# Loading the relative-position buckets of a decoder trunk: six wide transfers between weight units in place of twenty-four narrow ones

## The chip, the cores and the metric

The kernel runs on one core of a Trainium2 chip. A core has five engines with queues of their own: TensorE (PE in the profile; PEld is its weight load), VectorE (DVE), ScalarE (ACT), GpSimd (POOL) and SyncE (SP), which here only issues transfers. Transfers run on 16 DMA engines. The metric is the device time of one execution in microseconds; lower is better.

## The reference, cut to what matters

Two decoder layers run over 256 positions of width 1024, in float32. Layer 0 has differential attention with a relative-position bias, layer 1 latent attention; each is followed by a gated feed-forward part with a short convolution and by a gated embedding. The change touches the bias of layer 0 and two blocks of constants:

```python
bucket = t5_bucket(p_blk[:, :, None] - pos[:, None, :])      # 32 buckets
bias = jnp.take(rel_table, bucket, axis=0).astype(f32)       # table 32 x 8 heads
sc = jnp.where(causal_mask(i, s), sc + bias, NEG_INF)
```

For every pair of a query and a key a bucket number from 0 to 31 picks a row of a table with one value per head.

## The kernel before, in words

All weights lie in one array of units of 128 partitions x 1024 float32 (512 KB), in the order of use. `fetch` (L218) issues the next unit on SP's queue into a ring of five tiles (`st`, BUF_ST = 5). `split_unit` (L232) makes of each unit a high part (`wh`, ScalarE, L240) and the rest (`wl`, VectorE or GpSimd in turn, L241); four such pairs are held (BUF_W = 4). Every product is then three TensorE passes, hi*hi, hi*lo and lo*hi (`mm3`, L195 to L199). Counted from 0, units 0 and 1 are fetched in halves at the start; units 0 to 11 serve `proj_a(0)` and `proj_a(1)`, two units for each of q, k and v of a pair of heads; units 12 to 17 serve `proj_a(2)`, 18 to 23 `proj_a(3)`. The two tiles of `first_stats` (L656, from `in_xn`) take two places in the same ring, behind unit 3.

The bias: `bias_prep` (L377) computes the bucket numbers, 128 queries x 256 keys and 128 x 128, as bfloat16 and stores them in two arrays in DRAM, `s0` and `s1` (L421, L422). `bias_loads` (L435) reads them back as six pieces `oh` of 128 partitions x 2048 bfloat16 (512 KB): partition group j, 32 partitions, holds 4 KB of bucket numbers of query group j, the same in each of the 32 partitions. That is four transfers a piece, 24 in all (L445), each from one 4 KB row to 32 partitions. `bias_mm` (L448) compares each piece with the partition's own number (VectorE, L453), so that each partition marks its bucket, and multiplies with the table: 3 x 96 small products on TensorE (L460), copied to `bias` by ScalarE (L466). `attn_a` reads `bias` from its first head on.

Order: the program is traced in one order, in which `weave` mixes bias and attention with the projections by estimated TensorE time, and `later` runs a step once such an estimate has passed. A planner then orders each engine's queue: of what its own timeline holds ready it takes what was traced first. An engine takes its queue in that order and waits at the head of it. The constants of the convolutions (`cst[:, C_CONV[0]:]`, L668, 176 KB) and `grow` (L816, 384 KB) have no producer on the chip, so the planner put both on SP's queue early. The first are used in the feed-forward part of layer 0 (from L733 on), the second in layer 1.

Of the kernel before, what the change touches and what calls it, by code (L numbers as in the profile page):

```python
# [11 lines left out]
BF16 = mybir.dt.bfloat16  # L12
# [7 lines left out]
P = 128  # L20
# [26 lines left out]
C_CONV = (514, 690)  # L47
# [9 lines left out]
LAG = 6.0  # L57
# [38 lines left out]
def trunk(ctx, tc, xT, xN, pT, pos, consts, grow, wall, out):  # L96
    nc = tc.nc
# [4 lines left out]
    act = ctx.enter_context(tc.tile_pool(name="act", bufs=1))  # L102
# [50 lines left out]
    def later(lag, fn):  # L153
        late.append((clk[0] + lag, fn))
# [56 lines left out]
    cst = cp.tile([P, NCONST], F32, name="cst")  # L211
# [4 lines left out]
    turn = [0.0]  # L216
    share = [SH_A]

    def fetch(pieces=1):
        st = ring.tile([P, UNIT], F32, tag="st", name="st", bufs=BUF_ST)  # L220
        u, n = unit_no[0], UNIT // pieces
        unit_no[0] += 1
        for j in range(pieces):
            nc.sync.dma_start(st[:, j * n:(j + 1) * n], wall[u, :, j * n:(j + 1) * n])
            if pieces > 1:
                yield st
        if pieces == 1:
            yield st
# [19 lines left out]
    for i in range(2):  # L248
        pieces = fetch(2)
        for k in (4 * i, 4 * i + 2):  # L250
            nc.sync.dma_start(hT[:, k:k + 2], xT[:, k:k + 2])
            st = next(pieces)
# [131 lines left out]
    bst = {}  # L384

    def bias_prep():
        tb = []
        rest = col(C_REL, 32)
        for i in range(3):
            bt = ap_.tile([P, 32], BF16, name=f"tb{i}")  # L390
            V.tensor_copy(bt, rest)
            tb.append(bt)
            if i < 2:
                nr = ap_.tile([P, 32], F32, name=f"tr{i}")
                V.tensor_sub(nr, rest, bt)
                rest = nr
        bi = ap_.tile([P, 1], F32, name="bi")
        bidx = ap_.tile([P, 1], I32, name="bidx")
        G.iota(bidx, pattern=[[0, 1]], base=0, channel_multiplier=1)
        V.tensor_scalar(bidx, bidx, 31, None, ALU.bitwise_and)  # L400
        V.tensor_copy(bi, bidx)
        V.tensor_copy(posf, posi)

        identb = ap_.tile([P, P], BF16, name="identb")
        V.tensor_copy(identb, ident)
        dist = ap_.tile([P, 384], BF16, name="dist")
        V.tensor_scalar(dist[:, :S], posf[:, :S], posf[:, S:S + 1], 128.0, ALU.subtract, ALU.min)
        V.tensor_scalar(dist[:, S:], posf[:, P:S], posf[:, S + 1:S + 2], 128.0, ALU.subtract, ALU.min)
        pb = bankB()
        for j in range(len(THRESH) + 1):  # L410
            ge = ap_.tile([P, 384], BF16, tag="ge", name="ge", bufs=4)
            if j == 0:
                V.tensor_scalar(ge, dist, 0.0, 16.0, ALU.max, ALU.min)
            else:
                V.tensor_scalar(ge, dist, float(THRESH[j - 1]), None, ALU.is_ge)
            T.matmul(pb[:, :384], lhsT=identb, rhs=ge, start=j == 0, stop=j == len(THRESH))
        bkb = ap_.tile([P, 384], BF16, name="bkb")
        A.copy(bkb, pb[:, :384])
        s0 = dp.tile([P, S], BF16, name="s0")
        s1 = dp.tile([P, P], BF16, name="s1")  # L420
        nc.sync.dma_start(s0, bkb[:, :S])  # L421
        nc.sync.dma_start(s1, bkb[:, S:])  # L422
        bst["pcs"] = []
        later(LAG, lambda: bias_loads(s0, s1))
        bst["tb"], bst["bi"] = tb, bi
        ld = small(2)
        lscr = a_tile()
        for j in range(2):
            V.tensor_tensor_reduce(lscr[:, j * 64:(j + 1) * 64], col(C_LAM + 128 * j, 64),
                                   col(C_LAM + 128 * j + 64, 64), 1.0, 0.0, ALU.mult, ALU.add, ld[:, j:j + 1])  # L430
        le = small(2)
        A.activation(le, ld, AF.Exp)
        V.scalar_tensor_tensor(neglam, le[:, 1:2], -LAM_INIT, le[:, 0:1], ALU.add, ALU.subtract)

    def bias_loads(s0, s1):  # L435
        for kt, half in ((0, 0), (0, 1), (1, 0)):
            nq = 256 if kt == 0 else 128
            src = s0 if kt == 0 else s1
            ipp = 2048 // nq
            for pc in range(2):  # L440
                oh = act.tile([P, ipp, nq], BF16, tag="og", name="oh", bufs=8)
                i0 = half * 16 + pc * ipp
                row = src.rearrange("(j i) q -> j i q", i=32)[:, i0:i0 + ipp]
                for j in range(4):
                    nc.sync.dma_start(oh[j * 32:(j + 1) * 32], row[j:j + 1].broadcast_to([32, ipp, nq]))  # L445
                bst["pcs"].append(oh)

    def bias_mm():  # L448
        tb, bi = bst["tb"], bst["bi"]
        for n, (kt, half) in enumerate(((0, 0), (0, 1), (1, 0))):  # L450
            pcs = bst["pcs"][2 * n:2 * n + 2]
            for oh in pcs:
                V.tensor_scalar(oh, oh, bi, None, ALU.is_equal)  # L453
            yield 0.0
            for g in range(2):
                ps = bankB()
                for i in range(16):
                    lh = pcs[i // 8][:, i % 8, g * P:(g + 1) * P] if kt == 0 else pcs[g][:, i, :]
                    for z in range(3):
                        T.matmul(ps[:, i * 32:(i + 1) * 32], lhsT=lh, rhs=tb[z], start=z == 0, stop=z == 2)  # L460
                qt = g if kt == 0 else 1
                k0 = half * 16 if kt == 0 else g * 16
                off = 0 if qt == 0 else P + kt * P
                for j in range(4):
                    dst = bias[:, :, off + j * 32 + k0:off + j * 32 + k0 + 16]
                    A.activation(dst, ps.rearrange("p (i j h) -> p j h i", i=16, j=4)[:, j], AF.Copy, scale=-1.0)  # L466
                yield 1.2
        for off in (0, 2 * P):
            v = bias[:, :, off:off + P]
            G.affine_select(out=v, in_=v, pattern=[[0, HA], [-1, P]], compare_op=ALU.is_ge, fill=BIG, base=0,  # L470
                            channel_multiplier=1)
# [193 lines left out]

    run(proj_a(0))
    run(proj_a(1))
    nc.sync.dma_start(cst[:, C_CONV[0]:], consts[:, C_CONV[0]:])  # L668

    def ple_p(l):  # L670
        pst = d_tile()
# [136 lines left out]
    tabs = {}  # L808

    def layer_b_tables():  # L810
        bp = bctx.enter_context(tc.tile_pool(name="bpool", bufs=1))
        tabs["bp"] = bp
        bigm = bp.tile([P, 384], F32, name="bigm")
        tabs["bigm"] = bigm
        tabs["grow"] = bp.tile([P, 768], F32, name="grow")
        nc.sync.dma_start(tabs["grow"], grow)  # L816
        G.memset(bigm, 0.0)
        for off in (0, 2 * P):
            v = bigm[:, off:off + P]
            G.affine_select(out=v, in_=v, pattern=[[-1, P]], compare_op=ALU.is_ge, fill=BIG, base=0,  # L820
                            channel_multiplier=1)
        gqpe = bp.tile([P, 64], F32, name="gqpe")
        V.tensor_scalar(gqpe, col(C_QPE, 64), -SCALE_B, None, ALU.mult)
        ang = d_tile(64)
        for t in range(NT):
            V.tensor_scalar(ang[:, t * 32:(t + 1) * 32], col(C_FREQ, 32), posf[:, S + t:S + t + 1], None, ALU.mult)
        kk = d_tile(64)
        magic = 12582912.0
        V.tensor_scalar(kk, ang, 1.0 / (2.0 * math.pi), magic, ALU.mult, ALU.add)
        V.tensor_scalar(kk, kk, magic, None, ALU.subtract)  # L830
        c1 = 6.28125
        c2 = 0.00193500518798828125
        c3 = 2.0 * math.pi - c1 - c2
        for c in (c1, c2, c3):
            V.scalar_tensor_tensor(ang, kk, -c, ang, ALU.mult, ALU.add)
        V.tensor_scalar(ang, ang, math.pi, -math.pi, ALU.min, ALU.max)
        sn = d_tile(64)
        cs = d_tile(64)
        A.activation(sn, ang, AF.Sin)
        A.activation(cs, ang, AF.Sin, scale=0.5)  # L840
        V.tensor_mul(cs, cs, cs)
        V.tensor_scalar(cs, cs, -2.0, 1.0, ALU.mult, ALU.add)
        for nm, g in (("k", col(C_KPE, 64)), ("q", gqpe)):
            a = bp.tile([P, NT, 64], F32, name=f"ra{nm}")
            b = bp.tile([P, NT, 64], F32, name=f"rb{nm}")
            for t in range(NT):
                c_, s_ = cs[:, t * 32:(t + 1) * 32], sn[:, t * 32:(t + 1) * 32]
                V.tensor_mul(a[:, t, :32], g[:, :32], c_)
                V.tensor_mul(a[:, t, 32:], g[:, 32:], c_)
                V.scalar_tensor_tensor(b[:, t, :32], g[:, 32:], -1.0, s_, ALU.mult, ALU.mult)  # L850
                V.tensor_mul(b[:, t, 32:], g[:, :32], s_)
            tabs[nm] = (a, b)
# [13 lines left out]
    st = {}  # L866
# [417 lines left out]
```

## Time and profile before

| | us |
|---|---|
| median of 3 runs | 787.5 (785.61 to 788.36) |
| the profiled execution, its whole time | 789.36 |
| its span, first to last instruction | 787.6 |
| TensorE busy | 761.2 |
| VectorE busy | 561.2 |
| ScalarE busy | 483.8 |
| GpSimd busy | 296.0 |

The whole time of the profiled execution is 1.76 us more than its span and 1.86 us more than the median of the three runs. TensorE is the engine with the least idle time; the mean granted share of its clock over the span is 0.983. An instruction's row gives its start and its length in us, and in brackets how long its engine stood idle before it and which instruction or transfer ended that wait.

### The profile page before, as it was taken

Reading aid. Unit: us, or ns where it says so; the run is one execution under the profiler, and the core shown is the slowest. Engines: PE = TensorE matmul, PEld = TensorE weight load, DVE = VectorE, ACT = ScalarE, POOL = GpSimd, SP = SyncE. Lnnn points to the kernel's source line nnn. Section 1 sums busy time; section 2 is a strip of 40 time slices with the busy share of each in tenths; the row PEclk is TensorE's granted clock in tenths of the full one; section 3 lists DMA queues with packets and bytes.
Section 4 is the critical chain, followed back from the end, with each engine's and each line's share of the span. In section 5 each row is a group of like instructions: output and inputs, shape, how many; then the busy total and the mean of one; then the engine's idle time right before and its main releaser. Section 6 shows DMA issues by size and latency. Waiting matters only on the chain.

```text
span 787.6 us, 16504 instructions
## 1 busy us (share of the span) xinstructions
PE 761.2 (97%) x6396; PEld 748.7 (95%) x6396; DVE 561.2 (71%) x1142; ACT 483.8 (61%) x1040; POOL 296.0 (38%) x200
## 2 busy tenths in 40 slices
PE   8979999999999999998999899999899999999997
PEld 7979999999999999997989899999899999999997
DVE  6574888659978795538588987975558778775535
ACT  6535887666866665447766777564656666655443
POOL 2653355352332501145835646322523332301151
PEclk9989999999999999998999999999899999999999
DMA  8993345255656675554444323343455566565641
GB/s 310 256 273 100 108 148 162 81 187 161 191 185 191 191 240 197 180 169 134 153 143 135 107 81 108 108 133 108 146 156 188 182 187 184 171 202 176 184 130 55
DMA packets 37519, 127.97 MB, mean 162 GB/s; under 512 B 4672, under 2 KB 6208, under 8 KB 37440
## 3 DMA queue, kind: packets, MB, share of 16 engines
q1 hardware_dynamic: 36720, 126.38, 51.7%
q8 instruction: 50, 0.82, 0.4%
q10 hardware_dynamic: 720, 0.53, 0.2%
q14 instruction: 29, 0.24, 0.1%
HBM read 125.75 MB, written 1.15 MB: 161 GB/s over the span
## 4 chain that ended last, share of the span: by engine, by line
PE 83%; DVE 6%; DMA 4%; ACT 3%; POOL 2%; issue 2%; SPq 0%; POOLq 0%; ACTq 0%; DVEq 0%
PE pa L197 17%; PE pa L198 17%; PE pa L199 17%; PE pc L198 8%; PE pc L199 8%; PE pc L197 8%; DMA oh<-s 2%; DMA st<-in_wall 1%; POOL wl L241 1%; PE pb L198 1%; DVE wl L241 1%; PE pb L197 1%; PE pc L193 1%; PE pb L199 1%; PE pb L525 1%
## 5 line engine op out<-in xcount | busy, mean ns | idle before, releaser
L240 ACT CAST wh<-st 128x1024 fp32r<-128x1024 f32 x221 | 231.0, 1049 | 189.7 <-issue 68.0
L241 POOL TENSOR_TENSOR wl<-st,wh 128x1024 fp32r<-128x1024 f32 x74 | 180.4, 2438 | 245.8 <-ACT wh L240 226.3
L241 DVE TENSOR_TENSOR wl<-st,wh 128x1024 fp32r<-128x1024 f32 x147 | 189.8, 1291 | 87.2 <-ACT wh L240 86.9
L197 PE MATMUL pa<-hgH,wh 128*128 128x256 f32 x504 | 144.2, 286 | 2.2 <-ACT hgH L206 2.2
L198 PE MATMUL pa<-hgL,wh 128*128 128x256 f32 x504 | 144.2, 286 | 0.5 <-DVE hgL L207 0.3
L199 PE MATMUL pa<-hgH,wl 128*128 128x256 f32 x504 | 143.8, 285 | 0.0
L197 PE MATMUL pa<-wh,hgH 128*128 128x256 f32 x328 | 95.4, 296 | 7.4 <-DVE d L348 5.6
L197 PEld LDWEIGHTS pa<-hgH,wh 128*128 128x128 f32 x504 | 97.9, 194 | 2.6 <-ACT hgH L206 2.6
L198 PEld LDWEIGHTS pa<-hgL,wh 128*128 128x128 f32 x504 | 97.9, 194 | 1.1 <-DVE hgL L207 1.1
L199 PEld LDWEIGHTS pa<-hgH,wl 128*128 128x128 f32 x504 | 97.9, 194 | 0.0
L198 PE MATMUL pa<-wl,hgH 128*128 128x256 f32 x328 | 95.2, 291 | 1.2 <-DVE wl L241 0.6
L197 PE MATMUL pa<-og,wh 128*128 128x256 f32 x336 | 95.3, 287 | 0.0
L199 PE MATMUL pa<-wh,hgL 128*128 128x256 f32 x328 | 94.6, 290 | 0.5 <-DVE hgL L204 0.5
L198 PE MATMUL pa<-og,wh 128*128 128x256 f32 x336 | 95.1, 284 | 0.0
L199 PE MATMUL pa<-og,wl 128*128 128x256 f32 x336 | 94.9, 283 | 0.0
L198 PE MATMUL pc<-hgL,wh 128*128 128x256 f32 x328 | 93.8, 286 | 0.6 <-DVE hgL L207 0.5
L197 PE MATMUL pc<-hgH,wh 128*128 128x256 f32 x328 | 94.0, 287 | 0.1
L199 PE MATMUL pc<-hgH,wl 128*128 128x256 f32 x328 | 93.4, 285 | 0.0
L296 POOL TENSOR_TENSOR ssq<-ssq,d 128x256 f32<-128x256 f32 x35 | 33.6, 961 | 132.2 <-ACT d L295 131.7
L197 PEld LDWEIGHTS pa<-wh,hgH 128*128 128x128 f32 x328 | 63.9, 198 | 8.9 <-ACT bias L466 5.7
L198 PEld LDWEIGHTS pa<-wl,hgH 128*128 128x128 f32 x328 | 64.7, 197 | 2.1 <-DVE wl L241 1.0
L199 PEld LDWEIGHTS pa<-wh,hgL 128*128 128x128 f32 x328 | 64.6, 197 | 0.8 <-DVE hgL L204 0.7
(301 smaller groups left out, 1932.7 us busy)
## 6 DMA issues: line engine op xcount, KB each, us to landing
st<-in_wall SPq DMA_DIRECT2D x225, 512.0 KB, 3.6
oh<-s SPq DMA_DIRECT2D x24, 128.0 KB, 5.0
hT<-in_x SPq DMA_DIRECT2D x4, 256.0 KB, 4.8
st<-in_wall SPq DMA_DIRECT2D x4, 256.0 KB, 4.9
st<-in_xn SPq DMA_DIRECT2D x2, 512.0 KB, 6.9
d<-in_p SPq DMA_DIRECT2D x2, 256.0 KB, 4.0
out_h<-hT SPq DMA_DIRECT2D x4, 128.0 KB, 2.0
out_h<-hT ACTq DMA_DIRECT2D x4, 128.0 KB, 2.0
```

The source lines that it names most:

```text
L193: T.transpose(o, i, ident)
L197: T.matmul(ps, lhsT=aH, rhs=bH, start=start, stop=False)
L198: T.matmul(ps, lhsT=aH, rhs=bL, start=False, stop=False)
L199: T.matmul(ps, lhsT=aL, rhs=bH, start=False, stop=stop)
L240: A.copy(hi, st)
L241: eng.tensor_sub(lo, st, f(hi))
L296: G.tensor_add(sq, sq, t)
L525: T.matmul(pss[e][:, a:b], lhsT=x[rows, j, t * P:(t + 1) * P], rhs=y[rows, j, :b - a], start=start, stop=stop)
```

## The change

Each of the six pieces is loaded by one transfer instead of four: 128 partitions as destination, and as source four rows of 4 KB, each repeated 32 times. The pieces are no longer loaded by an estimated time: the fetches of units 12, 13 and 14 each call for two pieces, and `tc.issue_after` puts these on SP's queue behind that unit's transfer. `bias_mm` gives way in the trace until its pieces have been called for, so the first projection of `proj_a(2)` now stands ahead of it. The two blocks of constants are bound behind a unit's transfer in the same way: the convolutions' behind unit 18 (the 19th), `grow` behind the unit that was fetched last when `layer_b_tables` is traced, in the feed-forward part of layer 0.

```diff
     def fetch(pieces=1):
...
         for j in range(pieces):
-            nc.sync.dma_start(st[:, j * n:(j + 1) * n], wall[u, :, j * n:(j + 1) * n])
+            lastfetch[0] = nc.sync.dma_start(st[:, j * n:(j + 1) * n], wall[u, :, j * n:(j + 1) * n]).ins
+            if u in hooks:
+                hooks.pop(u)()
...
-        later(LAG, lambda: bias_loads(s0, s1))
+        for n, (kt, half) in enumerate(((0, 0), (0, 1), (1, 0))):
+            hooks[12 + n] = lambda src=(s0, s1)[kt], kt=kt, half=half: bias_loads(src, kt, half)
...
+    def bias_loads(src, kt, half):
+
+        nq = 256 if kt == 0 else 128
+        ipp = 2048 // nq
+        for pc in range(2):
+            oh = act.tile([P, ipp, nq], BF16, tag="og", name="oh", bufs=8)
+            i0 = half * 16 + pc * ipp
+            row = src.rearrange("(j i) q -> j i q", i=32)[:, i0:i0 + ipp]
+            with tc.issue_after(lastfetch[0]):
+                nc.sync.dma_start(oh.rearrange("p i q -> p (i q)"),
+                                  row.rearrange("j i q -> j (i q)").unsqueeze(1).broadcast_to([4, 32, 2048]))
+            bst["pcs"].append(oh)
+
+    def late_loads(dst, src):
+        with tc.issue_after(lastfetch[0]):
+            nc.sync.dma_start(dst, src)
...
         for n, (kt, half) in enumerate(((0, 0), (0, 1), (1, 0))):
+            while len(bst["pcs"]) < 2 * n + 2:
+                yield None
...
-    nc.sync.dma_start(cst[:, C_CONV[0]:], consts[:, C_CONV[0]:])
+    hooks[18] = lambda: late_loads(cst[:, C_CONV[0]:], consts[:, C_CONV[0]:])
...
-        nc.sync.dma_start(tabs["grow"], grow)
+        late_loads(tabs["grow"], grow)
```

## Rows read from the trace of the kernel before

**Rows 1.** The page: busy time of the engines, and packets of the transfers.
```profile
PE 761.2 (97%) x6396; PEld 748.7 (95%) x6396; DVE 561.2 (71%) x1142; ACT 483.8 (61%) x1040; POOL 296.0 (38%) x200
DMA packets 37519, 127.97 MB, mean 162 GB/s; under 512 B 4672, under 2 KB 6208, under 8 KB 37440
```

**Rows 2.** Stretches: length, PE, PEld, DVE, ACT, POOL busy, granted clock, DMA share, GB/s.
```profile
10.00:15.00 5.00, 4.54 (x37) 3.98 (x35) 4.16 (x20) 2.34 (x7) 0.00 (x0) 1.00 1.02 404
15.00:20.00 5.00, 3.50 (x22) 2.38 (x22) 3.72 (x13) 3.99 (x7) 3.56 (x1) 1.00 0.89 322
...
35.00:40.00 5.00, 5.00 (x45) 5.00 (x43) 1.23 (x2) 3.17 (x4) 1.59 (x2) 1.00 0.88 230
...
55.00:60.00 5.00, 2.55 (x12) 2.58 (x13) 3.84 (x5) 2.40 (x11) 3.93 (x2) 0.50 0.68 215
```

**Rows 3.** The chain of waits, 5 to 75 us: start, us, what.
```profile
29.27 6.13 DMA oh<-s
...
44.84 7.41 DMA st<-in_wall
...
53.40 3.31 DVE wl L241
56.70 0.61 DVE d L348
...
58.01 0.21 PE pa L198
...
61.17 0.12 PE pa L198
...
69.02 0.88 PE pb L525 x6
```

**Rows 4.** Instructions in order of time, 40 to 75 us.
```profile
47.76 1.05 ACT L240 CAST wh<-st 128x1024 fp32r<-128x1024 f32 x1 [8.40 <-DMA st<-in_wall]
...
48.85 1.23 DVE L241 TENSOR_TENSOR wl<-st,wh 128x1024 fp32r<-128x1024 f32 x1 [0.36 <-ACT wh L240]
...
49.31 2.55 PE L460 MATMUL pb<-tb,oh 128*128 128x32 bf16 x96
...
50.05 0.75 DVE L453 TENSOR_SCALAR oh<-oh,bi 128x2048 bf16<-128x2048 bf16 x1
...
57.45 0.55 PE L197 MATMUL pa<-wh,hgH 128*128 128x256 f32 x1 [5.58 <-DVE d L348]
```

**Rows 5.** SP's queue in order of time, 0 to 75 us.
```profile
26.95 1.79 SPq L224 DMA_DIRECT2D st<-in_wall  x2
28.80 12.75 SPq L445 DMA_DIRECT2D oh<-s  x20
41.70 0.35 SPq L224 DMA_DIRECT2D st<-in_wall  x1
...
44.30 27.88 SPq L224 DMA_DIRECT2D st<-in_wall  x9
```

**Rows 6.** GpSimd in order of time, 25 to 40 us.
```profile
28.70 2.40 POOL L241 TENSOR_TENSOR wl<-st,wh 128x1024 fp32r<-128x1024 f32 x1
33.03 2.41 POOL L241 TENSOR_TENSOR wl<-st,wh 128x1024 fp32r<-128x1024 f32 x1 [1.93 <-ACT wh L240]
```

**Rows 7.** VectorE in order of time, 25 to 40 us.
```profile
31.17 1.22 DVE L241 TENSOR_TENSOR wl<-st,wh 128x1024 fp32r<-128x1024 f32 x1 [1.71 <-ACT wh L240]
```

**Rows 8.** Transfers by line: count, KB each, median us from issue to landing.
```profile
st<-in_wall SPq DMA_DIRECT2D x225, 512.0 KB, 3.6
oh<-s SPq DMA_DIRECT2D x24, 128.0 KB, 5.0
```

**Rows 9.** The pieces' own instructions: ns min/median/max, first and last start.
```profile
L453 DVE TENSOR_SCALAR oh<-oh,bi x6: 737/752/2283, 36.6 to 50.0; 128x2048 bf16<-128x2048 bf16 x6
```

**Rows 10.** TensorE in order of time, 14 to 21 us: its waits.
```profile
15.32 0.39 PE L197 MATMUL pa<-wh,hgH 128*128 128x256 f32 x1 [0.78 <-ACT wh L240]
...
19.91 0.39 PE L198 MATMUL pa<-wl,hgH 128*128 128x256 f32 x1 [0.55 <-POOL wl L241]
```

More of the change, by code (lines that the diff above doesn't have):

```diff
@@ L217, in trunk @@
     share = [SH_A]
+    hooks, lastfetch = {}, [None]
     def fetch(pieces=1):
@@ L433, in bias_prep @@
         V.scalar_tensor_tensor(neglam, le[:, 1:2], -LAM_INIT, le[:, 0:1], ALU.add, ALU.subtract)
[L435 to L446, printed above, removed]
+    def bias_loads(src, kt, half):
[12 more added lines that the diff above has]
+            nc.sync.dma_start(dst, src)
     def bias_mm():
```

## The prediction

> **What bounds the kernel now.** I read the page first: TensorE is busy 761.2 us of a span of 787.6 [rows 1], so a change off TensorE gains only where TensorE stands idle or runs at a low clock. The TensorE rows in order of time show where that is near this change: the one long wait of the first 75 us is 5.58 us ahead of the products at 57.45 [rows 4]. Next I read the granted clock by stretches: 0.50, the 1.2 GHz level, from 55 to 60 against 1.00 before [rows 2]; it fell in that wait, and the first products behind it take 0.21 us a step, those from 61.17 on 0.12 [rows 3]. Last, the chain of waits says why: the pieces' transfers, then a weight unit that took 7.41 us to land, its subtraction on VectorE (3.31) and behind that an evacuation (0.61) for which TensorE waited [rows 3]. The same delay is seen on ScalarE, which stood 8.40 us for the transfer of unit 12 before its cast at 47.76 [rows 4].
>
> SP's queue gives the reason. It issued units 10 and 11 from 26.95, then twenty of the pieces' transfers from 28.80 to 41.55, and only then unit 12; units from 13 on follow at 44.30 [rows 5]. Unit 12's place in the ring was free long before: it takes that of unit 7, whose subtraction ended at 28.70 + 2.40 = 31.10 [rows 6]. The 24 narrow transfers took 15 us of the queue, and in that stretch the DMA engines were busy 0.88 of the time for 230 GB/s, while weights and inputs ran at 404 GB/s [rows 2].
>
> **The change part by part, against the profiled execution (789.36 us whole, span 787.6; the median of the runs is 1.86 lower, so differences are carried over to 787.5).**
>
> *What goes.* Unit 12 ahead of the pieces takes away the wait of 5.58 and the half clock. From 57.45 eighteen steps ran before full speed; at 0.21 to 0.22 for 0.12 a step, 3.95 us in place of 2.15, that is 1.8. So 7.4 us can go. Also 18 issues go from SP's queue; SP only issues, so this counts only through what lands sooner.
>
> *What is added: the wide transfers' own time.* A packet here is 4 KB (a partition's row of a unit or of a piece). At 404 GB/s and share 1.02, an engine moves 404 / 16.3 = 24.8 GB/s, 165 ns a packet; in the pieces' stretch 230 / 14.1 = 16.3 GB/s, 251 ns [rows 2]. A wide transfer has 128 packets. How they are dealt to engines no row shows. All transfers before were dealt to 16: the profile lists 276, and of the 4672 packets under 512 B [rows 1] 256 are data (128 rows of 44 B, 128 of 256 B), which leaves 4416 = 16 x 276 completion marks. But each of these has 128 or 32 as its outermost count on both sides; the new source has 4, each row repeated 32 times, against 128 partitions. So the bounds are: 16 engines with 8 packets each (1.3 us at 165, 2.0 at 251) and 4 engines with one row's 32 copies each (5.3 us, 8.0). I take 4 engines, since what both sides can be cut into without cutting the source's outer dimension is 4, and 165 ns, since four engines draw only 99 GB/s, below the 230 that the pieces reached. The outer count decides, I think, and there the 24 old transfers are no near row.
>
> A rule of the Trainium skill bears on this (DMA: Bandwidth & Descriptors, section "Why a DMA increments its semaphore by 16 and not by 1"): the number of engines is the largest up to 16 that divides the slowest dimension of both access patterns, and on such queues they are the lowest-numbered ones. By it the new transfer has 4 engines; the trace agrees as far as it goes, with 16 marks for each transfer of 128 or 32 rows, and has no outer count of 4.
>
> *Where that time lies.* With five ring tiles unit 12 issues at 31.1, unit 13 behind unit 8's subtraction (31.17 + 1.22 = 32.4 [rows 7]), unit 14 behind unit 9's (33.03 + 2.41 = 35.4 [rows 6]). The pieces stand between them: two behind each. A unit lands 3.6 us after issue [rows 8], 1.3 of it packets; I put 1.15 of the rest ahead and 1.15 behind. On the four engines, each in order: unit 12 until 33.6; pieces 1 and 2 (2 x 5.3) until 44.2; unit 13 until 45.5, landed 46.7; pieces 3 and 4 until 56.1, landed 57.2; unit 14 landed 58.5; piece 5 landed 63.8, piece 6 69.1; unit 15 landed 70.5. So each unit now waits for pieces on a quarter of the engines.
>
> TensorE is through with units up to 11 at about 49.5 (its first third of the bias products starts at 49.31 [rows 4]). Units 12 and 13: 48 steps of 0.12, until 55.3. First bias products (2.55 [rows 4]): 57.8. Second: compare 0.75 [rows 9] behind 57.2, idle 0.2, until 60.5. Unit 14: cast 1.05 and subtraction 1.23 [rows 4] behind 58.5, idle 0.3, until 63.7. Third bias products: first half idle 0.85, until 65.8; second half idle 4.0 for piece 6, until 71.1; unit 15 (1.05 and 2.41 on GpSimd) at 74.0, idle 2.9. Sum 8.3. One head's scores need no bias, two times 0.88 us [rows 3], and fit in: 6.5. If more work stands there, or products start on the high part alone, it falls to 3. Of the half clock I take 0.5 between 0 and 1.8: gaps of 0.55 to 0.78 us, three of them [rows 10], went by at a clock of 1.00 [rows 2], the 5.58 did not. Total: 6.5 + 0.5 - 7.4 = **-0.4**, from -4.4 to +2.7.
>
> *The constants.* 560 KB leave SP's queue at about 10 us, 1.4 us of transfer at 404 GB/s. TensorE's three waits there (the first 0.78, the last 0.55) are for the splitting of units 2 and 3 [rows 10], which were issued ahead of both blocks, so I count 0 (bounds 0 and -1.0). At their new places they are one unit's worth of transfer each at most, long before their use: 0, and at most their 1.4 us if a unit is late just there.
>
> *Order.* The compares and bias products are the same in number; they are traced behind the first projection of `proj_a(2)`. TensorE's total work doesn't change, so this costs nothing by itself (bounds -1 and +1 for heads that finish earlier or later). Behind a compare that waits for its piece stand, on VectorE, subtractions and evacuations: the second rival.
>
> **The rivals.** *All 16 engines (0.31).* Then a piece takes 1.3 to 2.0 us, the ten transfers from unit 12 to unit 15 end at 32.3 + 4 x 1.3 + 6 x 2.0 = 49.5 at the latest, and unit 15 is wanted only from 63 on. Unit 12 is cast as soon as a pair is free, nothing is late next, and 6.4 to 7.4 go: about 7, **780.5**. For it: every transfer listed used 16; against it: the outer count of 4.
>
> *VectorE stuck behind a compare (0.27), the slower side.* An engine takes its queue in order. Before, five of the six compares stood ahead of unit 12's subtraction: it started at 48.85, the last compare at 50.05 [rows 4], the first at 36.6 [rows 9]. The planner places them where it believes the pieces landed. If it believes in fast pieces and they come over four engines, unit 12 waits for a piece. This decides from a landing later than 49.5 - 0.75 - 1.23 = 47.5 of any piece compared ahead of that subtraction. For the fourth (57.2) TensorE starts unit 12 at 59.2: idle 9.7, plus 1.8, less 7.4: +4.1, 791.6. For the fifth (63.8): 65.8, idle 16.3, +10.7, 798.2. I put it at **795**. For it: the five of six; against it: each pair of pieces is now issued behind a unit, which puts it later in the planner's eyes too.
>
> That the pieces don't come to stand between the units would need an earlier free place than 31.1 for three units; the ring has none.
>
> **How the numbers follow.** Forecast 0.42, the rivals 0.31 and 0.27. The forecast is 787.5 - 0.4 = **787.1**, alone from 783 to 790.3. 0.3% is 2.4 us, about what a measurement of this kernel can tell from no change. Below 785.1: nearly all of the first rival (0.30) and a fifth of the forecast (0.08), 0.38. Above 789.9: nearly all of the second (0.26) and a tenth of the forecast (0.04), 0.30; between, 0.32. The range goes from 779 to 798: it leaves out the second rival's fifth piece and beyond, and packets of 251 ns on four engines.
>
> **What would show it.** Packets under 512 B: 24 transfers go and 6 come, 4672 - 384 + 24 = 4312 with four engines, 4384 with sixteen. The pieces' landing: 6 us and more with four, near 4 with sixteen. In the changed trace ScalarE's wait before unit 12 is gone in all cases but the second rival's; under the forecast there are waits for transfers at about 64 to 74, and the clock shows 0.50 there at most briefly. A TensorE row without a wait over 1 us between 45 and 80 makes the forecast wrong; a wait at 49 to 66 whose releaser is VectorE's subtraction behind a compare shows the second rival.

## The result, and the profile after

The changed kernel takes **806.84 us** (median of 4 runs, 802.61 to 808.17) against 786.56 for the kernel before (4 runs, 783.71 to 788.36): a ratio of 1.0252, interval 1.0202 to 1.0302. It is 20 us slower; 787.1 was forecast and the range ended at 798. The profiled execution took 806.75 us, its span is 804.9.

From the page of the changed kernel, beside [rows 1, 8]: busy time of the engines, the packets, and the row of the weight units' transfers (count, KB each, median us from issue to landing).

```profile
PE 767.5 (95%) x6396; PEld 752.7 (94%) x6396; DVE 560.3 (70%) x1142; ACT 482.3 (60%) x1040; POOL 296.9 (37%) x200
...
DMA packets 37159, 127.97 MB, mean 159 GB/s; under 512 B 4312, under 2 KB 5848, under 8 KB 37080
...
st<-in_wall SPq DMA_DIRECT2D x225, 512.0 KB, 3.6
```

The 4312 small packets are the count that the prediction gave for four engines. By the Trainium skill (DMA: Bandwidth & Descriptors, section "Why a DMA increments its semaphore by 16 and not by 1") an outermost count of 4, against 128 on the other side, gives four engines, and the trace agrees. The weight units' median of 3.6 us has not moved: a few late units of 225 don't show in a median, so the rows in order of time have to be read.

The span is 17.3 us longer: TensorE is busy 6.3 us more with the same 6396 products (the clock), and idle 11.0 more. The stretches of the changed kernel show where (columns as in [rows 2]: length, PE, PEld, DVE, ACT, POOL busy, granted clock, DMA share, GB/s):

```profile
45.00:50.00 5.00, 1.75 (x8) 1.75 (x9) 3.21 (x5) 1.11 (x2) 0.40 (x1) 0.65 0.29 102
50.00:55.00 5.00, 5.00 (x32) 5.00 (x32) 0.92 (x1) 0.42 (x1) 3.58 (x2) 0.67 0.26 105
55.00:60.00 5.00, 1.33 (x12) 1.13 (x10) 1.47 (x2) 0.00 (x0) 0.00 (x0) 1.00 0.66 191
60.00:65.00 5.00, 3.92 (x19) 3.93 (x20) 1.61 (x3) 1.05 (x1) 0.00 (x0) 0.51 1.01 252
...
70.00:75.00 5.00, 0.07 (x1) 0.00 (x0) 2.09 (x3) 0.78 (x1) 0.47 (x1) 0.88 0.26 104
```

From 45 to 55 and from 70 to 75 the DMA engines have a share of 0.26 to 0.29 and move 102 to 105 GB/s. That is four of sixteen, each at about 105 / 4 = 26 GB/s: the pieces, and what stands among them on those four, are under way, and the share leaves nothing for the other twelve. From 40 to 75 TensorE is busy for 19.9 us of 35, where it was busy for 29.4 before.

TensorE's waits, and what it does behind the last (start, us; in brackets the idle time before and its releaser), beside the one wait of 5.58 in [rows 4]:

```profile
48.25 0.58 PE L198 MATMUL pa<-wl,hgH 128*128 128x256 f32 x1 [5.46 <-DVE wl L245]
...
61.08 1.12 PE L193 MATMUL pt<-ident,d 128*128 128x128 f32 x4 [4.74 <-DVE d L352]
...
75.54 1.09 PE L193 MATMUL pt<-ident,d 128*128 128x128 f32 x4 [5.46 <-DVE d L352]
76.69 2.72 PE L471 MATMUL pb<-tb,oh 128*128 128x32 bf16 x96
79.25 0.56 PE L197 MATMUL pa<-wh,hgH 128*128 128x256 f32 x1
```

VectorE, to which all three waits point:

```profile
40.14 0.95 DVE L464 TENSOR_SCALAR oh<-oh,bi 128x2048 bf16<-128x2048 bf16 x1 [6.02 <-DMA oh<-s]
46.31 0.75 DVE L464 TENSOR_SCALAR oh<-oh,bi 128x2048 bf16<-128x2048 bf16 x1 [5.22 <-DMA oh<-s]
46.98 1.22 DVE L245 TENSOR_TENSOR wl<-st,wh 128x1024 fp32r<-128x1024 f32 x1
...
53.20 0.92 DVE L464 TENSOR_SCALAR oh<-oh,bi 128x2048 bf16<-128x2048 bf16 x1 [3.68 <-DMA oh<-s]
58.53 0.75 DVE L464 TENSOR_SCALAR oh<-oh,bi 128x2048 bf16<-128x2048 bf16 x1 [4.41 <-DMA oh<-s]
59.20 1.22 DVE L245 TENSOR_TENSOR wl<-st,wh 128x1024 fp32r<-128x1024 f32 x1
60.34 0.68 DVE L352 TENSOR_TENSOR d<-pa,s 128x512 f32<-128x512 f32 x1
...
67.93 0.75 DVE L464 TENSOR_SCALAR oh<-oh,bi 128x2048 bf16<-128x2048 bf16 x1 [6.32 <-DMA oh<-s]
...
72.91 0.75 DVE L464 TENSOR_SCALAR oh<-oh,bi 128x2048 bf16<-128x2048 bf16 x1 [4.15 <-DMA oh<-s]
73.58 1.22 DVE L245 TENSOR_TENSOR wl<-st,wh 128x1024 fp32r<-128x1024 f32 x1
```

Each compare (L464) waits for its piece, 29.8 us in all, and behind the second, fourth and sixth stands a subtraction that TensorE needs (units 10, 12 and 14). So the waits look like VectorE's doing. ScalarE's casts tell of the units, though:

```profile
49.38 1.04 ACT L244 CAST wh<-st 128x1024 fp32r<-128x1024 f32 x1
60.82 1.05 ACT L244 CAST wh<-st 128x1024 fp32r<-128x1024 f32 x1 [10.40 <-DMA st<-in_wall]
74.22 1.05 ACT L244 CAST wh<-st 128x1024 fp32r<-128x1024 f32 x1 [12.35 <-DMA st<-in_wall]
```

Units 14 and 15 are cast at 60.82 and 74.22, the moment they land. SP's queue (beside [rows 5]) says how that comes about:

```profile
28.71 0.33 SPq L226 DMA_DIRECT2D st<-in_wall  x1
29.09 1.23 SPq L449 DMA_DIRECT2D oh<-s  x2
32.37 0.34 SPq L226 DMA_DIRECT2D st<-in_wall  x1
32.74 4.34 SPq L449 DMA_DIRECT2D oh<-s  x2
37.18 5.31 SPq L226 DMA_DIRECT2D st<-in_wall  x1
42.54 1.64 SPq L449 DMA_DIRECT2D oh<-s  x2
48.22 13.18 SPq L226 DMA_DIRECT2D st<-in_wall  x4
```

Unit 12 is issued at 28.71, ahead of all pieces. But unit 14's issue alone takes 5.31 us in place of 0.33, and unit 15's, begun at 48.22, takes 8.07 (the longest of its line), to 56.29. The chain of waits of the changed kernel (start, us, what) runs through just these two transfers, a piece issued at 32.74 and then unit 15, 25.89 us from issue to landing, and not through a compare. Behind them come unit 15's cast on ScalarE, an evacuation that stood behind this cast in ScalarE's queue (of transposes that TensorE had done by 62.2), a step of VectorE, and the first bias products:

```profile
32.74 15.48 DMA oh<-s
48.22 25.89 DMA st<-in_wall
74.22 1.05 ACT wh L244
75.26 0.59 ACT qk L206
75.88 0.76 DVE qk L207
76.69 2.72 PE pb L471 x96
```

### The profile page after: what moved, and what is told of

It reads as the page before. It is cut to its first block, busy times and chain, and to the rows that moved or that the text cites. A ratio compares the mean times of both kernels' runs of the same rounds, so it can differ in the third digit from the quotient of the medians.

```text
span 804.9 us, 16446 instructions
## 1 busy us (share of the span) xinstructions
PE 767.5 (95%) x6396; PEld 752.7 (94%) x6396; DVE 560.3 (70%) x1142; ACT 482.3 (60%) x1040; POOL 296.9 (37%) x200
## 2 busy tenths in 40 slices
DMA packets 37159, 127.97 MB, mean 159 GB/s; under 512 B 4312, under 2 KB 5848, under 8 KB 37080
## 4 chain that ended last, share of the span: by engine, by line
PE 82%; DMA 7%; DVE 4%; ACT 3%; POOL 2%; issue 2%; SPq 0%; POOLq 0%; ACTq 0%; DVEq 0%
PE pa L197 17%; PE pa L198 17%; PE pa L199 17%; PE pc L198 8%; PE pc L199 8%; PE pc L197 8%; DMA st<-in_wall 4%; DMA oh<-s 2%; POOL wl L245 1%; PE pb L198 1%; DVE wl L245 1%; PE pb L197 1%; PE pc L193 1%; PE pb L199 1%; PE pb L536 1%
## 5 line engine op out<-in xcount | busy, mean ns | idle before, releaser
L278 POOL TENSOR_TENSOR s<-s,neghalf 128x4 f32<-128x4 f32 (+2 forms) x30 | 41.4, 1379 | 80.3 <-DVE s L344 51.7
```

The source lines that it names most:

```text
L278: G.tensor_tensor(dst, src, neghalf[:, :n], ALU.pow)
```

## The experiments

The theory from these rows: the pieces go over four engines one after the other, a quarter of every unit stands behind them there, and units 13 to 15 are late. Rivals: the new order is what costs; VectorE's queue, with compares that wait, is what costs; the late constants cost. Line numbers in the rows are those of the kernel that each comes from.

**Sixteen engines, all else as changed.** The bucket of a partition is numbered 4b + j instead of 32j + b, so that the source can have the 32 copies outermost. The same bytes go in the same six transfers; the table's rows are arranged to fit.

```diff
-        V.tensor_scalar(bidx, bidx, 31, None, ALU.bitwise_and)
+        V.tensor_scalar(bidx, bidx, 2, None, ALU.logical_shift_right)
...
-                                  row.rearrange("j i q -> j (i q)").unsqueeze(1).broadcast_to([4, 32, 2048]))
+                                  row.rearrange("j i q -> j (i q)").unsqueeze(0).broadcast_to([32, 4, 2048]))
...
-        cst[j * 32:(j + 1) * 32, C_REL + j * 8:C_REL + (j + 1) * 8] = f("rel_bias_table")
+        cst[j::4, C_REL + j * 8:C_REL + (j + 1) * 8] = f("rel_bias_table")
```

> The changed kernel with one thing different: partition 4 b + j of a piece holds query group j and bucket b (before: 32 j + b), so that the source of each wide transfer has 32 as its outermost count (each time all four rows) in place of 4; the table's rows and the bucket numbers follow. Theory A (four engines: the loss comes from pieces that run over 4 engines, and from VectorE's queue waiting at the compares for them): 16 engines, 4384 packets under 512 B, pieces land within about 4 us, the compares no longer wait over 1 us, TensorE has none of the three waits near 48, 61 and 75 us, and the time is 777 to 784 us, below the kernel before. Theory B (the order: pieces between units and bias products behind the first projection of proj_a(2) are what costs): packets may change, the time stays at 800 us and more.

Measured: 782.32 us (10 runs, 781.59 to 786.23), ratio to the kernel before 0.9964 (0.9945 to 0.9983): 24 us below the changed kernel by one exchange of two dimensions. Its packets on the page:

```profile
DMA packets 37231, 127.97 MB, mean 164 GB/s; under 512 B 4384, under 2 KB 5920, under 8 KB 37152
```

Its casts of units 14 and 15 on ScalarE:

```profile
46.88 1.05 ACT L244 CAST wh<-st 128x1024 fp32r<-128x1024 f32 x1 [2.79 <-PE pa L199]
48.37 1.05 ACT L244 CAST wh<-st 128x1024 fp32r<-128x1024 f32 x1 [0.43 <-PE pa L199]
```

4384 is sixteen engines. Unit 15 is cast at 48.37 instead of 74.22, and both casts wait for a free pair behind TensorE, no longer for a transfer; the compares wait 1.7 us for their pieces, and TensorE has no wait over 0.5 us from 28 to 105. The number of engines is the cause. Missed: the pieces land 7.8 us after issue (median), not within about 4, as they queue behind one another. Not foreseen: waits of 0.92 and 0.89 near 110, and behind them a granted clock of 0.66 from 110 to 115.

**Four engines in the old order.** The kernel before with the wide transfers alone:

```diff
-                for j in range(4):
-                    nc.sync.dma_start(oh[j * 32:(j + 1) * 32], row[j:j + 1].broadcast_to([32, ipp, nq]))
+                nc.sync.dma_start(oh.rearrange("p i q -> p (i q)"),
+                                  row.rearrange("j i q -> j (i q)").unsqueeze(1).broadcast_to([4, 32, 2048]))
```

> The kernel before with the wide transfers alone (outermost count 4, six in place of 24), in its own order, pieces ahead of unit 12, constants early. Theory A: six pieces of 5.1 us in a row on four engines, from about 30 to 61 us, unit 12 lands behind most of them, and TensorE stands from about 50 to 60 or more: 793 to 805 us. Theory B: no slower than the kernel before, 784 to 788 us, since the order is that of before.

Measured: 801.77 us (4 runs, 800.09 to 802.48), ratio 1.0208 (1.0175 to 1.024). Its longest wait on TensorE:

```profile
70.53 1.11 PE L193 MATMUL pt<-ident,d 128*128 128x128 f32 x4 [17.00 <-DVE d L348]
```

ScalarE's cast of unit 12:

```profile
70.37 1.05 ACT L240 CAST wh<-st 128x1024 fp32r<-128x1024 f32 x1 [17.88 <-DMA st<-in_wall]
```

And SP's queue:

```profile
28.50 16.71 SPq L444 DMA_DIRECT2D oh<-s  x6
45.31 33.70 SPq L224 DMA_DIRECT2D st<-in_wall  x9
```

Six issues take 16.71 us here, where twenty narrow ones took 12.75 [rows 5]; unit 12, issued at 45.31, lands at 70.4, behind all six pieces, and TensorE stands 17.00 us. So the wide transfers alone cost 15 us in the old order; the changed kernel lost 20.

**The new order with narrow transfers.** The changed kernel with four transfers of 32 partitions a piece:

```diff
-                nc.sync.dma_start(oh.rearrange("p i q -> p (i q)"),
-                                  row.rearrange("j i q -> j (i q)").unsqueeze(1).broadcast_to([4, 32, 2048]))
+                for j in range(4):
+                    nc.sync.dma_start(oh[j * 32:(j + 1) * 32], row[j:j + 1].broadcast_to([32, ipp, nq]))
```

> The changed kernel with four narrow transfers for each piece, as in the kernel before; order, hooks and late constants as changed. Theory A: all transfers over 16 engines, 779 to 785 us, somewhat over the wide ones with an outermost count of 32, since 24 narrow transfers run at 251 ns a packet. Theory B: 800 us and more.

Measured: 787.72 us (10 runs, 785.37 to 790.23), ratio 1.0023 (1.0002 to 1.0043). My 779 to 785 missed by 3 us. The order does not cost 20 us, but it brings nothing with narrow pieces either. Rows of its TensorE:

```profile
50.72 1.07 PE L193 MATMUL pt<-ident,d 128*128 128x128 f32 x4 [1.98 <-DVE d L352]
...
59.68 0.63 PE L193 MATMUL pt<-ident,d 128*128 128x128 f32 x4 [1.01 <-DVE d L352]
```

The wait of 5.58 has become two of 2.99 in all, again of VectorE behind compares (9.1 us of waits for pieces), and near 115 the same two short waits (0.83, 0.90) as in the first experiment follow.

**The late constants alone.** The kernel before, with the two blocks bound behind units 18 and later:

```diff
-    nc.sync.dma_start(cst[:, C_CONV[0]:], consts[:, C_CONV[0]:])
+    hooks[18] = lambda: late_loads(cst[:, C_CONV[0]:], consts[:, C_CONV[0]:])
...
-        nc.sync.dma_start(tabs["grow"], grow)
+        late_loads(tabs["grow"], grow)
```

> The kernel before with the late constants alone (behind unit 18, and grow behind the unit fetched last). Theory A: within 2 us of the kernel before, 784.5 to 788.5 us; the first 26 us may be 0.5 us shorter. Theory C (the constants' new places hold SP's queue or the engines up): 795 us and more.

Measured: 785.75 us (10 runs, 783.86 to 791.02), ratio 0.9993 (0.9966 to 1.0019): no difference, as expected. In its profile the wait of 5.58 has nonetheless given way to one of 1.71 (at 60.32, the clock at 0.50 from 60.4 to 63.8), because the planner's order shifted with the edit: all 24 narrow transfers now go out in one row from 27.24. That execution took 785.59, 3.8 less than the profiled one of before; the medians of 10 and 25 runs lie 0.5 apart, and the 789.36 of the profiled one is near the upper end of those 25 (782.63 to 789.90), so at least part of the 3.8 is the scatter of single runs.

**VectorE freed of the waiting compares.** This tells VectorE's queue from the engines. The changed kernel, four engines, but each compare bound behind a subtraction of a later unit on VectorE:

```diff
-            while len(bst["pcs"]) < 2 * n + 2:
+            while unit_no[0] < 14 + 2 * n:
...
-                V.tensor_scalar(oh, oh, bi, None, ALU.is_equal)
+                with tc.issue_after(lastsub[0]):
+                    V.tensor_scalar(oh, oh, bi, None, ALU.is_equal)
```

> The changed kernel, pieces still over four engines, with the compares bound behind VectorE's subtraction of unit 12, 14 and 16 (pair by pair) and traced that much later. Theory A1 (most of the 20 us is VectorE's queue: a compare that waits for its piece holds up subtractions and evacuations behind it): the compares wait under 5 us in all (29.8 in the changed kernel), TensorE idles about 6 us less, and the time is 785 to 793 us. Theory A2 (the four engines alone cost it, since weight units come behind pieces on them, and the order on VectorE hardly counts): 798 us and more.

Measured: 816.24 us (4 runs, 812.9 to 820.09), ratio 1.0366 (1.0324 to 1.0408). The compares waited 3.1 us instead of 29.8, and it is 9 us slower still. Its casts of units 13 to 15 on ScalarE:

```profile
50.90 1.04 ACT L244 CAST wh<-st 128x1024 fp32r<-128x1024 f32 x1 [6.78 <-DMA st<-in_wall]
63.21 1.04 ACT L244 CAST wh<-st 128x1024 fp32r<-128x1024 f32 x1 [11.27 <-DMA st<-in_wall]
77.67 1.04 ACT L244 CAST wh<-st 128x1024 fp32r<-128x1024 f32 x1 [13.42 <-DMA st<-in_wall]
```

And its longest waits on TensorE:

```profile
67.49 1.11 PE L193 MATMUL pt<-ident,d 128*128 128x128 f32 x4 [8.56 <-DVE d L354]
...
78.77 0.58 PE L197 MATMUL pa<-wh,hgH 128*128 128x256 f32 x1 [5.00 <-ACT wh L244]
```

VectorE's subtraction of unit 14, behind which the evacuation for the first of these waits stands:

```profile
64.28 1.23 DVE L245 TENSOR_TENSOR wl<-st,wh 128x1024 fp32r<-128x1024 f32 x1 [13.92 <-ACT wh L244]
```

Units 13, 14 and 15 are as late as in the changed kernel or later (77.67 against 74.22), and TensorE now waits for them: 8.56 us for what stands on VectorE behind unit 14, then 5.00 for unit 15. So taking the compares' waits away wins nothing on four engines, and the theory that they are the cause, with its 785 to 793, falls. What they cost in the changed kernel's own order is not shown by this, since the edit also moves the bias products back in TensorE's queue. The further 9 us come late: the last bias products start at 99.2 (90.6 in the changed kernel), and the granted clock is 0.50 from 138.4 to 158.8. I take that for the price of moving the bias back; it was not tested by itself.

**Sixteen engines in the old order.** The kernel before with the exchange of the first experiment, none of the new order, constants as before (the source in the form [32, 4, 2048], the shift and the table's rows as there).

> The kernel before with six wide transfers whose source has an outermost count of 32, and nothing else of the change: its own order, constants early. If the width over 16 engines is what helps and the new order is not: 778 to 784 us, as the same transfers in the new order (782.3) or better. If the new order (pieces between units) is needed: 785 to 788 us, since all pieces still stand ahead of unit 12.

Measured: **780.01 us** (5 runs, 779.61 to 783.07), ratio 0.9931 (0.9905 to 0.9957), the fastest of all. SP's queue:

```profile
28.61 4.62 SPq L444 DMA_DIRECT2D oh<-s  x6
33.33 44.83 SPq L224 DMA_DIRECT2D st<-in_wall  x13
```

Six issues in 4.62 us let unit 12 out at 33.33 instead of 41.70, without any order written by hand. The pieces are also through sooner. The stretch in which the last four land (columns as before):

```profile
39.00:44.00 5.00, 5.00 (x44) 5.00 (x43) 4.22 (x6) 0.78 (x2) 2.38 (x2) 1.00 1.03 419
```

With the engines as busy (1.03), the 24 narrow transfers of the fourth experiment moved 242 GB/s from 32 to 45. ScalarE casts unit 12 at 44.90 (47.76 before) and unit 14 at 47.49 (52.32 before). So one wide transfer for four narrow ones is a gain, as long as it runs on sixteen engines. TensorE has no wait over 0.5 us from 28 to 150, so the two near 110 are missing as well.

**The same with the late constants.** The edits of the last and of the fourth experiment together.

> As the kernel before with wide transfers of outermost count 32 in its own order, and the constants late. Constants late: 0 to 1 us below the same kernel with constants early; 777 to 784 us, the version that could beat the others if the old trace order keeps TensorE busier around 115 us.

Measured: 784.43 us (12 runs, 781.78 to 788.97), ratio 0.9974 (0.9953 to 0.9995), against an expected 777 to 784, a narrow miss. Its profile follows that of the last kernel to about 350 us and loses 3.4 us between 382 and 410, in layer 1: TensorE waits 0.55 and 1.72 us near 396 (0.69 in the last kernel), and the clock is at 0.50 from 397.6 to 401.0. The fourth experiment's profile, late constants in the same old order, has the same 0.55 and 1.72 near 398 and a clock of 0.50 behind them; no kernel in the new order has them. Why was not taken apart. So the late constants bring nothing, and may cost up to 4 us.

## Why the prediction was wrong, step by step

**Right.** What bounds the kernel and what can go: 7.4 us were named, and with the pieces over sixteen engines the median falls by 6.3 in the old order and by 4.0 in the new one (780.0 and 782.3; the first rival, sixteen engines, said 780.5). By 160 us the same count of products stands 7.6 us earlier in the profile of the old order on sixteen engines than in that of the kernel before. How much of the 7.4 a usual execution of the kernel before loses is not shown: the fourth experiment's profile has lost most of that wait too, and its median fell by only 0.5. Four engines: 4312. A piece's time of 5.3 us: the fourth compare follows the third by 58.53 - 53.20 = 5.33, the sixth the fifth by 72.91 - 67.93 = 4.98. Landings on the four engines: fourth piece 58.5 (57.2 forecast), unit 14 60.8 (58.5), sixth piece 72.9 (69.1), unit 15 74.2 (70.5). The last ones are 4 us late, about what piece 5 lost: it came 9.4 us after piece 4. From 60 to 65 all sixteen engines were busy (1.01) for 252 GB/s, which is 252 / 16.2 = 15.6 GB/s an engine or 263 ns a packet, and at that a piece's 32 packets take 8.4 us; while only four engines were at work (0.26, 105 GB/s) it was 162 ns. So the 165 ns of the working held there, and not while units ran on the other twelve. In the second experiment, too, piece 5 came 8.9 us after piece 4. The working also lacked SP's held issues.

**Wrong, the main step: what TensorE does meanwhile.** The forecast said that TensorE "is through with units up to 11 at about 49.5", and then filled the gaps with units 12 and 13 and the bias products: 8.3 us idle, 6.5 with a head's scores. The first part failed because compares 1 and 2 stand ahead of the subtraction of unit **10** on VectorE, two units earlier than the forecast looked: TensorE stands still until 48.25 and ends unit 11 at 56.34. The second part failed because a queue is fixed: the first bias products stand on TensorE ahead of unit 14's (from 79.25), but behind transposes that waited for VectorE until 75.54, and by the chain of waits they were released by the evacuation behind unit 15's cast on ScalarE and a step of VectorE. So not one of the 288 starts before 76.69, though four pieces had been compared by 59.3. Idle was 5.46 + 4.74 + 5.46 = 15.7 where 6.5 was forecast.

**Wrong, the clock.** 0.5 us were taken for the half clock. In each of the three waits the granted clock fell to 0.50 and stayed there for 6.8 us, as stretches of the changed kernel cut to it show:

```profile
46.50:53.30 6.80, 5.05 (x23) 5.05 (x24) 3.12 (x6) 1.53 (x2) 3.70 (x2) 0.50 0.26 98
60.10:66.90 6.80, 5.83 (x28) 5.83 (x28) 1.51 (x3) 1.05 (x1) 0.00 (x0) 0.50 0.97 240
73.80:80.60 6.80, 5.00 (x106) 4.76 (x107) 5.29 (x8) 5.53 (x10) 2.98 (x2) 0.50 0.58 189
```

In them 23, 24 and 6 steps took 5.06 + 5.20 + 1.40 = 11.7 us, where 53 steps of 0.12 take 6.4; with some 0.5 for the transposes and bias products beside them that is 5.8. The two terms together, (15.7 - 5.6) of idle time and (5.8 - 1.8) of clock, give 14.1; 840 products into its work TensorE is at 90.4 before and at 104.4 after, 14.0 apart, though not quite the same products are done by then.

**Wrong, the place where the working ended.** The sum ended at 74 us. The heads, whose bias comes later, come later too: near 131 to 139 TensorE waits 0.89, 0.88 and 1.17 us, the clock falls once more (0.50 from 138.6 to 142.0), and by 160 us the same count of products stands 19.8 us later; 2.3 come back until the end.

**The rivals.** The second rival named the releaser that the trace shows in all three waits, VectorE's work behind a compare, and priced it at 4 to 11 us for one hit on unit 12. It hit three times. As a cause it is not enough: with those waits taken away on four engines, unit 15 is cast at 77.67 and nothing is won. The point that decides is the transfer's outermost count: with 32 the same order, the same compares and the same six transfers give 782.3. The forecast for the order (0, within 1) was roughly right with narrow pieces (ratio 1.0023); on sixteen engines the order and the late constants together measured 782.3 against 780.0 without them, with overlapping intervals, so a loss of 2 us is likely but not shown. The constants' 0 held (0.9993).

Left open: why a packet took 263 ns while units and pieces kept all engines busy from 60 to 65, and why the late constants bring the loss near 396 in the old order.

## What to carry to other kernels

Before merging narrow broadcast loads into one, look at the outermost count of source and destination: count the small packets, or read the DMA share while only that load runs (0.26 here is four of sixteen), and put a long dimension outermost (32 and 128 ran on sixteen engines here, 4 on four), by renumbering partitions if need be. On sixteen engines the merge paid: 419 GB/s in place of 242. A transfer on few engines delays everything queued behind it on those engines, even when the rest stand idle, so price it by the last neighbour to land and not by its own bytes. And don't fill a forecast gap with work that stands behind it in the engine's queue: read where the planner put that work.

## What the runs showed of the hardware that was not expected

- SP's issue of a transfer is not always short. With the pieces on four engines the longest issue of a weight unit took 7.82 us in the old order, 8.07 in the changed kernel and 12.04 with the compares put back; in the six kernels with all transfers on sixteen it took 0.78 to 1.61. SP was held while four engines were behind and twelve mostly idle (share 0.26 from 50 to 55 in the changed kernel).
- Four engines moved 102 to 105 GB/s, about 26 each, close to the 24.8 an engine worked out from 404 GB/s on all sixteen [rows 2]: here an engine was hardly faster with the others idle. With all sixteen busy on units and pieces it was slower, 15.6 (252 GB/s at 1.01, from 60 to 65).
- In and behind a wait of 4.7 to 5.6 us TensorE had 6.8 us at a granted clock of 0.50 (the 1.2 GHz level), three times in the changed kernel and once before; the wait of 17.00 us in the old order had 17.1 us of it.
